# Column tiles of one width in the expert stage, and the groups of experts dealt anew

## The chip, the cores and the metric

One core of one Trainium2 chip runs the whole program. The metric is device time in microseconds, the median of three runs: 1858.34 us (1855.30 to 1859.64) before the change. All times below are us unless marked ns. TensorE (PE) does the matmuls, VectorE (DVE), ScalarE (ACT) and GpSimd (POOL) the rest, and SyncE (SP) issues the transfers from HBM, each engine in the order of its own queue.

## The reference, cut to what matters

The reference is one block of a network on 512 tokens of width 1024: a differential attention and a state-space branch side by side, their merge, and then a mixture of 64 experts. Only the last stage is changed. Every token goes to two experts, and each expert has 6 MB of float32 weights, 402.7 MB in all.

```python
MOE_EXPERTS, MOE_TOP_K, MOE_HIDDEN = 64, 2, 512
g_sel = jnp.argmax(g_logits, axis=-1)                    # one of 8 groups of experts
top_v, top_i = lax.top_k(e_sel_logits, MOE_TOP_K)        # two experts of that group
...
def expert_block(args):
    xblk, e = args
    hid = jax.nn.silu(xblk @ w_gate[e]) * (xblk @ w_up[e])
    return hid @ w_down[e]
...
out = jnp.zeros((n_tok, d), jnp.float32).at[buf_tok].add(yb.astype(jnp.float32) * buf_w[:, None])
return rms_norm(x + out, final_norm_w, NORM_EPS)
```

## The kernel before

The first 850 us are projections, attention and the state-space branch. Then the router runs, and the expert stage follows.

*Slots and groups.* Each expert gets a fixed number of slots, columns of the 128 columns of a tile, for the tokens sent to it. Experts 0 to 2 (`NS = 3`, L1202) keep their place; the other 61 are sorted on the chip by their number of tokens, fullest first, and the sorted order is the table `perm`. Places below `NW = 12` are wide and get 64 slots, the others 32 (`width`, L1214). Experts are dealt into groups that fill 128 slots (L1208 to L1212): the first is `[0, 1]`, two wide ones; then follow 18 groups, of kind T (one wide, two narrow) or F (four narrow) as the string at L1210 says. Tokens beyond an expert's slots would be done in a loop at the end (L1839), which runs as often as the tables of `overflow_tables` (L1646) say.

*One group.* `gather` (L1683) collects the group's tokens with one-hot matmuls, for two groups at a time, after the gate and up projections of every second group. `gate_up` (L1708) runs over eight k (128 rows of the weight each) and two halves (gate, up), and in each such step has one matmul for each expert of the group: the stationary operand is the expert's slots (32 or 64 columns), the moving one 512 columns of its weights. An expert's matmul uses only its own columns of the array. `down` (L1732) does the same over four k and two halves. A float32 matmul stands as two records in the trace. `combine` (L1761) adds the result of the group before into the output rows, and `slots` (L1693) makes the tables that this needs.

*Weights and buffers.* A weight tile is 128 x 2048 float32, 1 MB; an expert has four for gate and up (`gu`) and two for down (`dn`). The list `tiles` (L1223 to L1227) is the order in which they are loaded: by group, and in it all gate and up tiles before the down tiles. `fill` (L1605) issues the next tiles of the list on SP while there is room: 17 buffers of the pool `big`, one `ewx` and one pair of `stg`; from group 1 on two of `big` hold the output rows (`room["big"] -= 2`, L1806). After every second k the group's tiles of these two k are freed, and `fill` runs again. SP issues in that order, and a transfer whose buffer is still in use holds up all behind it.

*The start of the stage.* The weights of experts 0 to 2, 18 tiles, need no routing and are issued while the last projection runs. For all others SP reads the place from `perm` (`source`, L1234), which VectorE writes at the end of the router (L1595). On the way there, `rk` (L1490) builds the first group's one-hot matrix `P0` (L1497), in two rounds of two chunks.

Of the kernel before, what the change touches and what calls it, by code (L numbers as in the profile page):

```python
# [14 lines left out]
OP = mybir.AluOpType  # L15
# [103 lines left out]
def block_kernel(ctx: ExitStack, tc: tile.TileContext, I, out):  # L119
# [1079 lines left out]

    NS, NW = 3, 12  # L1202
    narrow = iter(range(NW, 64))

    def some(n):
        return [next(narrow) for _ in range(n)]

    groups = [[0, 1]]  # L1208
    wide = list(range(2, NW))
    for kind in "TFTFTTFTFTFTTFTFTF":  # L1210
        groups.append([wide.pop(0)] + some(2) if kind == "T" else some(4))
    NG = len(groups)  # L1212

    def width(e):  # L1214
        return 64 if e < NW else 32

    def spans(g_):
        o = 0
# [3 lines left out]

    tiles = []  # L1223
    for g_ in groups:
        first = [e for e in g_ if e < NS]
        for es in (first, g_[len(first):]):
            tiles += [("gu", e, q) for q in range(4) for e in es] + [("dn", e, q) for q in range(2) for e in es]  # L1227
    wt = {}
    nxt = {"i": 0, "end": False}
    LASTN = 4  # L1230
# [212 lines left out]
    def route(cl, prev):  # L1443
        cs = slice(cl[0], cl[-1] + 1)
        n = len(cl)
        g = lambda k: R[k][:, cs]

        def r1():
            gl = lg[:, cs, 0:8]
            first("gm", "og", lambda c: lg[:, c, 0:8], gl)  # L1450

        def r2():
            el = lg[:, cs, 8:72].rearrange("p c (g e) -> p c g e", g=8)
            V.tensor_tensor(R["et"][:, cs], el, og4(cs), op=OP.mult)
            V.tensor_reduce(g("es"), R["et"][:, cs].rearrange("p c g e -> p c e g"), axis=AX.X, op=OP.add)

        def first(m, o, row, rows):
            V.tensor_reduce(g(m), rows, axis=AX.X, op=OP.max)
            for c in cl:
                V.scalar_tensor_tensor(R["d1"][:, c], row(c), R[m][:, c:c + 1], rev8, op0=OP.is_equal, op1=OP.mult)  # L1460
            V.tensor_reduce(g("gx"), g("d1"), axis=AX.X, op=OP.max)
            V.tensor_tensor(g(o), g("d1"), b8(g("gx")), op=OP.is_equal)

        def r3():
            first("m1", "o1", lambda c: R["es"][:, c], g("es"))

        def r4():
            V.scalar_tensor_tensor(g("es"), g("o1"), NEG, g("es"), op0=OP.mult, op1=OP.add)
            first("m2", "o2", lambda c: R["es"][:, c], g("es"))

        def r5():
            V.tensor_tensor(g("d1"), g("o1"), g("o2"), op=OP.add)
            V.tensor_tensor(R["ab"][:, cs], og4(cs), g("d1")[:, :, None, :].to_broadcast([128, n, 8, 8]), op=OP.mult)

        def abf(c):
            return R["ab"][:, c].rearrange("p g e -> p (g e)")

        def rank():
            if cl[0] == 0:
                R["rps"] = side()  # L1480
            rps = R["rps"]
            for c in cl:
                for cc in range(c):
                    T.matmul(rps[:, c * E:c * E + E], lhsT=onesb, rhs=abf(cc), start=(cc == 0), stop=False)
                T.matmul(rps[:, c * E:c * E + E], lhsT=triS, rhs=abf(c), start=(c == 0), stop=True)
            if cl[-1] == NCH - 1:
                for c in range(NCH):
                    T.matmul(rps[:, 256:256 + E], lhsT=onesb, rhs=abf(c), start=(c == 0), stop=(c == NCH - 1))

        def rk():  # L1490
            V.scalar_tensor_tensor(rk1[:, cs].rearrange("p c e -> p (c e)"), R["rps"][:, cl[0] * E:cl[-1] * E + E], 1.0,
                                   R["ab"][:, cs].rearrange("p c g e -> p (c g e)"), op0=OP.add, op1=OP.mult)
            if cl[0] == 0:
                R["P0"] = mt("P", [128, NCH, 256], "P")[:, :, :128]
            for c in cl:
                for e in range(2):
                    V.tensor_scalar(R["P0"][:, c, 64 * e:64 * e + 64], iota1, rk1[:, c, e:e + 1], fst[:, 3, c:c + 1],  # L1497
                                    op0=OP.is_equal, op1=OP.mult)

        def gat(k):  # L1500
            if cl[0] == 0:
                gb[k] = side()
            gather_mm(R["P0"], gb[k][:, :128], k, cl)

        deps = [lgj[c] for c in cl]
        pr = 0.15 if not prev else 0.3
        j = J("V", 1.2, r1, deps + ([rtj] if not prev else []), prio=pr)
        r["gd", cl[0]] = j
        j = J("V", 0.6, r2, [j, r.get("et")], prio=pr)
        r["et"] = j  # L1510
        j = J("V", 1.2, r3, [j], prio=pr)
        j = J("V", 1.4, r4, [j], prio=pr)
        m2j.append(j)
        j = J("V", 0.45, r5, [j], prio=pr)
        kw = None
        if prev:
            kw = J("P", 0.214 * KW, lambda: keep_warm(KW), [lmj[3]], prio=10, acq=["s"], rel=["s"], lag=0.2)
        rj = J("P", 0.1, rank, [j, prev, kw], prio=1, acq=["s"] if not prev else [], lag=0.2)
        if cl[-1] == NCH - 1:
            J("P", 0.9, lambda: keep_warm(4), [rj], prio=1, acq=["s"], rel=["s"])  # L1520
        kj = J("V", 0.2 + 0.35 * n, rk, [rj, r.get("rk")], prio=pr)
        r["rk"] = kj
        last = cl[-1] == NCH - 1
        for k0 in (0, 1):
            j = J("P", 0.22 * n, lambda k0=k0: gat(k0), [kj, lmj[3], r.get(("g", k0))],
                  prio=2 if last else 10, acq=["s"] if not prev else [], lag=0.2)
            r["g", k0] = j
        return rj, kj
# [117 lines left out]
    def overflow_tables():  # L1646

        ex = mt("y", [128, 1024], "ex")
        ext, pe, pf, ef = (ex[:, i * E:i * E + E] for i in range(4))
        io = ex[:, 320:352]  # L1650
        cm = R["cnt"]
        V.tensor_scalar(cm[:, :NW], cm[:, :NW], 64.0, None, op0=OP.subtract)
        V.tensor_scalar(cm[:, NW:], cm[:, NW:], 32.0, None, op0=OP.subtract)
        V.tensor_scalar(ext, cm, 0.0, None, op0=OP.is_gt)
        for m in range(1, 8):
            V.scalar_tensor_tensor(ext, cm, 64.0 * m, ext, op0=OP.is_gt, op1=OP.add)
        a, b = ext, pe
        for sft in (1, 2, 4, 8, 16, 32):
            V.tensor_copy(b[:, :sft], a[:, :sft])
            V.tensor_tensor(b[:, sft:], a[:, sft:], a[:, :E - sft], op=OP.add)  # L1660
            a, b = b, (pf if b is pe else pe)
        V.tensor_scalar(io, iota1[:, :32], -1.0, None, op0=OP.add)
        V.memset(ef, 0.0)
        V.tensor_copy(ef[:, 0:1], a[:, E - 1:E])
        le = mt("y", [128, 16, E], "le")
        bs = R["base"]
        for i in range(2):
            m = slice(16 * i, 16 * i + 16)
            V.tensor_tensor(le, a[:, None, :].to_broadcast([128, 16, E]),
                            io[:, m].unsqueeze(2).to_broadcast([128, 16, E]), op=OP.is_le)  # L1670
            V.tensor_reduce(ef[:, 1 + 16 * i:17 + 16 * i], le, axis=AX.X, op=OP.add)
            V.tensor_tensor(le, le, ext[:, None, :].to_broadcast([128, 16, E]), op=OP.mult)
            V.tensor_reduce(bs[:, m], le, axis=AX.X, op=OP.add)
        em = ef[:, 1:33]
        V.tensor_tensor(bs, io, bs, op=OP.subtract)
        V.tensor_scalar(em, em, float(E - 1), None, op0=OP.min)
        V.tensor_scalar(io, em, NW - 0.5, 32.0, op0=OP.is_lt, op1=OP.mult)
        V.tensor_scalar(io, io, 32.0, None, op0=OP.add)
        V.scalar_tensor_tensor(bs, bs, 64.0, io, op0=OP.mult, op1=OP.add)
        V.tensor_copy(R["ovi"], ef)  # L1680

# [11 lines left out]
    def slots(P, es, wcols):  # L1693
# [11 lines left out]
            V.tensor_scalar(sl[r], ws[r, e:e + 1], 0.5, None, op0=OP.mult)  # L1705
        return pt, sl

    def gate_up(xt, es, gu, done=lambda k: None, pre=lambda k: None):  # L1708
        W = es[-1][1].stop
        pg, pu = gps.tile([128, 512], F32, name="g"), gps.tile([128, 512], F32, name="g")  # L1710
        for k in range(8):
            pre(k)
            for i, o in enumerate((pg, pu)):
                for e, r in es:
                    T.matmul(o[r], lhsT=xt[:, k, r], rhs=gu(e, k)[:, i * 512:i * 512 + 512],  # L1715
                             start=(k == 0), stop=(k == 7), tile_position=(0, r.start))
            done(k)
# [14 lines left out]
    def down(ht, es, dn, done=lambda k: None):  # L1732
        ps = [side(), side()]
        for k in range(4):
            for i in range(2):
                for e, r in es:
                    T.matmul(ps[i][r], lhsT=ht[:, k, r], rhs=dn(e, k)[:, i * 512:i * 512 + 512],  # L1737
                             start=(k == 0), stop=(k == 3), tile_position=(0, r.start))
            done(k)
# [38 lines left out]
    for gi, g_ in enumerate(groups):  # L1778
# [37 lines left out]
        if gi == 3:  # L1816
            overflow_tables()
        pt, sl = ps_
        if gi % 2:
            ps_ = group_slots(P, gi + 1)  # L1820
            if not last and gi + 2 < NG:
                P = onehot(groups[gi + 2:gi + 4])
        elif gi and not last:
            xt = rows(256)
            gather(P, xt)
            ps_ = group_slots(P, gi + 1)
        yps = down(ht, es, wk("dn"), done("dn"))
        if gi == 0:
# [163 lines left out]
```

## Time and profile before

| | |
|---|---|
| median of three runs | 1858.34 us (1855.30 to 1859.64) |
| profiled execution, its own time | 1855.86 us |
| span of that execution | 1854.1 us |
| mean granted clock of TensorE | 0.987 |
| PE busy | 1792.5 us (97%) |
| DVE busy | 794.3 us (43%) |
| ACT busy | 422.2 us (23%) |
| read from HBM | 471.04 MB |

The profile is one execution on the chip. It lists busy times, the span in 40 equal slices of 46.35 us with the busy share in tenths, who waited for whom, and the costliest groups of instructions; the trace behind it gives single instructions and any stretch of time. Matmuls are pipelined, so a busy TensorE is not one at its peak.

### The profile page before, as it was taken

How to read it: one execution, taken by the hardware profiler on the slowest of the kernel's cores; microseconds unless marked ns; L12 is line 12 of the kernel's file. 1: busy time of each engine (PE TensorE's matmuls, PEld its weight loads, DVE VectorE, ACT ScalarE, POOL GpSimd, SP SyncE). 2: the span in 40 equal slices, each digit the busy share in tenths (PEclk: the TensorE clock that was granted, in tenths of full speed). 3: DMA queues.
4: the chain of work that ended last, by engine and by line, in shares of the span. 5: the costliest groups of instructions: out<-in, count | busy, mean ns of one | idle time of the engine just before them, and what ended most of it. 6: DMA issues, size and time to landing. Idle time of an engine off the chain costs nothing. (4 is left out here: it accounts for less than half of the span.)

```text
span 1854.1 us, 23043 instructions
## 1 busy us (share of the span) xinstructions
PE 1792.5 (97%) x8767; PEld 1034.0 (56%) x8767; DVE 794.3 (43%) x1566; ACT 422.2 (23%) x869; POOL 317.6 (17%) x329
## 2 busy tenths in 40 slices
PE   8999999999999999999999999999999999998995
PEld 6877788878787777886424242342424242432432
DVE  7698832587877865324121512121121211212122
ACT  4355530344443432121101010000101010100101
POOL 5244421253635342100000000000000000000001
PEclk8999999999999999999999999999999999999998
DMA  5311122212122123369689999989999999999996
GB/s 158 101 63 52 47 91 91 80 58 91 61 77 74 64 71 100 103 248 367 245 313 421 420 420 420 420 339 421 420 420 420 420 421 415 374 420 420 421 420 255
DMA packets 81472, 474.66 MB, mean 256 GB/s; under 512 B 10192, under 2 KB 10576, under 8 KB 35664
## 3 DMA queue, kind: packets, MB, share of 16 engines
q1 hardware_dynamic: 81360, 473.17, 64.7%
q8 instruction: 70, 1.15, 0.2%
q14 instruction: 42, 0.34, 0.0%
HBM read 471.04 MB, written 2.10 MB: 255 GB/s over the span
## 5 line engine op out<-in xcount | busy, mean ns | idle before, releaser
L1715 PE MATMUL g<-ew,xt 128*32 128x512 f32 (+1 forms) x1904 | 460.3, 603 | 13.4 <-DMA ew<-in_gu_dram 13.3
L243 PE MATMUL g<-hH,w 128*128 128x512 f32 x1024 | 345.7, 401 | 0.0
L1715 PEld LDWEIGHTS g<-ew,xt 128*32 128x32 f32 (+1 forms) x1904 | 91.9, 114 | 348.5 <-issue 319.0
L1737 PE MATMUL s<-ew,hT 128*32 128x512 f32 (+1 forms) x968 | 245.2, 634 | 13.4 <-DMA ew<-in_dn_dram 12.0
L243 PEld LDWEIGHTS g<-hH,w 128*128 128x128 f32 x1024 | 192.4, 188 | 43.7 <-issue 6.0
L243 PE MATMUL g<-hL,w 128*128 128x512 f32 x512 | 199.9, 390 | 0.0
L1720 DVE SCALAR_TENSOR_TENSOR hh<-hh,g 128x512 f32<-128x512 f32 x19 | 13.1, 687 | 407.3 <-ACT hh L1719 407.3
L1894 POOL TENSOR_TENSOR fst<-fst 128x1 f32<-128x1 f32 x4 | 1.2, 302 | 987.8 <-ACT fo L1887 987.6
L203 DVE TENSOR_TENSOR w<-stg,w 128x1024 fp32r<-128x1024 f32 x108 | 141.9, 1322 | 55.4 <-ACT w L200 32.2
L1737 PEld LDWEIGHTS s<-ew,hT 128*32 128x32 f32 (+1 forms) x968 | 49.2, 119 | 193.7 <-issue 150.9
L1436 PE MATMUL s<-P,x 128*128 128x256 f32 (+1 forms) x640 | 136.3, 372 | 0.0
L1436 PEld LDWEIGHTS s<-P,x 128*128 128x128 f32 x640 | 117.3, 192 | 20.8 <-issue 5.7
L1747 DVE SCALAR_TENSOR_TENSOR yl<-s,sl,yh 128x512 fp32r<-128x512 f32 x38 | 28.3, 750 | 201.6 <-ACT yh L1746 201.0
L198 POOL TENSOR_SCALAR w<-stg 128x1024 fp32r<-128x1024 f32 x60 | 70.8, 1180 | 253.9 <-DMA stg<-in_wu_dram 169.8
L1719 ACT ACTIVATE hh<-g 128x512 f32<-128x512 f32 x19 | 11.3, 597 | 425.1 <-PE g L1715 425.1
L243 PEld LDWEIGHTS g<-hL,w 128*128 128x128 f32 x512 | 96.4, 188 | 16.8
L848 DVE SCALAR_TENSOR_TENSOR xb<-u,cw,xb 128x511 f32<-128x511 f32 (+2 forms) x96 | 81.7, 861 | 23.4 <-ACT xb L844 21.7
L1759 DVE TENSOR_TENSOR acc<-acc,s 128x512 f32<-128x512 f32 x144 | 87.6, 679 | 8.1 <-PE s L1754 8.1
L243 PE MATMUL g<-w,hH 128*128 128x512 f32 x256 | 84.5, 411 | 0.0
L1746 ACT ACTIVATE yh<-s,sl 128x512 fp32r<-128x512 f32 x38 | 26.0, 687 | 253.9 <-PE s L1737 253.6
L200 ACT ACTIVATE w<-stg 128x1024 fp32r<-128x1024 f32 x60 | 63.2, 1053 | 75.4 <-DMA stg<-in_wu_dram 52.8
L243 PE MATMUL g<-sH,w 128*128 128x512 f32 x256 | 79.9, 393 | 0.0
(332 smaller groups left out, 2385.6 us busy)
## 6 DMA issues: line engine op xcount, KB each, us to landing
ew<-in_gu_dram SPq DMA_DIRECT2D x238, 1024.0 KB, 17.4
ew<-in_dn_dram SPq DMA_DIRECT2D x117, 1024.0 KB, 17.6
stg<-in_wu_dram SPq DMA_DIRECT2D x120, 512.0 KB, 3.6
stg<-in_gu_dram SPq DMA_DIRECT2D x36, 512.0 KB, 17.3
stg<-in_dn_dram SPq DMA_DIRECT2D x14, 512.0 KB, 17.4
xT<-in_xT_dram SPq DMA_DIRECT2D x4, 512.0 KB, 5.7
x<-in_xn_dram SPq DMA_DIRECT2D x2, 1024.0 KB, 11.2
ew<-in_dn_dram SPq DMA_DIRECT2D x4, 512.0 KB, 13.7
```

Of the source, the lines that this page charges most:

```text
L198: G.tensor_scalar(c["h"], c["st"], 1.0, 0.0, op0=OP.mult, op1=OP.add)
L200: A.activation(c["h"], c["st"], AF.Copy)
L203: (G if i % 10 == 9 else V).tensor_tensor(c["lo"], c["st"], c["h"].bitcast(F32), op=OP.subtract)
L243: T.matmul(cell[b], lhsT=x, rhs=y, start=first and i == 0, stop=last and i == 2)
L848: V.scalar_tensor_tensor(x()[:, 3 - k:], t["u"][:, :n], w[:, k:k + 1], x()[:, 3 - k:], op0=OP.mult, op1=OP.add)
L1436: T.matmul(o, lhsT=x1(c)[:, d], rhs=P[:, c], start=(c == 0), stop=(c == NCH - 1))
L1715: T.matmul(o[r], lhsT=xt[:, k, r], rhs=gu(e, k)[:, i * 512:i * 512 + 512], start=(k == 0), stop=(k == 7), tile_position=(0, r.start))
L1720: V.scalar_tensor_tensor(hh, hh, 1.0, pg[:W], op0=OP.add, op1=OP.mult)
L1737: T.matmul(ps[i][r], lhsT=ht[:, k, r], rhs=dn(e, k)[:, i * 512:i * 512 + 512], start=(k == 0), stop=(k == 3), tile_position=(0, r.start))
L1746: A.activation(yh[:, i], ps[i][:W], AF.Copy, scale=sl[:, :1])
L1747: V.scalar_tensor_tensor(yl[:, i], ps[i][:W], sl[:, :1], yh[:, i].bitcast(F32), op0=OP.mult, op1=OP.subtract)
L1759: V.tensor_tensor(res(c)[:, h], src(c)[:, h], ps, op=OP.add)
```

## The change

Five wide places fewer, and another shape of matmul. `NW` becomes 10, the first group holds experts 0, 1 and 2, of which only expert 0 is wide, and the rest is dealt as seven T and ten F groups, so there are 18 groups instead of 19 and eight wide experts instead of twelve. A new function `parts` cuts every expert's columns into pieces of 32, so a wide expert has two matmuls per step, on the same weights, where it had one; a group always has four matmuls of 32 columns per step. The list of tiles no longer sets the fixed experts apart, the one-hot matrix of the first group is built for three experts, and the overflow tables learn which places are wide. The last group is now one of odd number, so the gather ahead of it is for one group alone.

```diff
-    NS, NW = 3, 12
+    NS, NW = 3, 10
...
-    groups = [[0, 1]]
-    wide = list(range(2, NW))
-    for kind in "TFTFTTFTFTFTTFTFTF":
+    groups = [[0, 1, 2]]
+    wide = list(range(NS, NW))
+    for kind in "FTFTFFTFTFFTFTFTF":
         groups.append([wide.pop(0)] + some(2) if kind == "T" else some(4))
...
     def width(e):
-        return 64 if e < NW else 32
+        return 64 if e == 0 or NS <= e < NW else 32
...
     for g_ in groups:
-        first = [e for e in g_ if e < NS]
-        for es in (first, g_[len(first):]):
-            tiles += [("gu", e, q) for q in range(4) for e in es] + [("dn", e, q) for q in range(2) for e in es]
+        tiles += [("gu", e, q) for q in range(4) for e in g_] + [("dn", e, q) for q in range(2) for e in g_]
...
             for c in cl:
-                for e in range(2):
-                    V.tensor_scalar(R["P0"][:, c, 64 * e:64 * e + 64], iota1, rk1[:, c, e:e + 1], fst[:, 3, c:c + 1],
+                for e, r_ in spans(groups[0]):
+                    V.tensor_scalar(R["P0"][:, c, r_], iota1[:, :width(e)], rk1[:, c, e:e + 1], fst[:, 3, c:c + 1],
                                     op0=OP.is_equal, op1=OP.mult)
...
-        V.tensor_scalar(cm[:, :NW], cm[:, :NW], 64.0, None, op0=OP.subtract)
-        V.tensor_scalar(cm[:, NW:], cm[:, NW:], 32.0, None, op0=OP.subtract)
+        V.tensor_scalar(cm, cm, 32.0, None, op0=OP.subtract)
+        for a_, b_ in ((0, 1), (NS, NW)):
+            V.tensor_scalar(cm[:, a_:b_], cm[:, a_:b_], 32.0, None, op0=OP.subtract)
...
+    def parts(es):
+
+        return [(e, slice(o, o + 32)) for e, r in es for o in range(r.start, r.stop, 32)]
+
     def gate_up(xt, es, gu, done=lambda k: None, pre=lambda k: None):
...
-                for e, r in es:
+                for e, r in parts(es):
                     T.matmul(o[r], lhsT=xt[:, k, r], rhs=gu(e, k)[:, i * 512:i * 512 + 512],
                              start=(k == 0), stop=(k == 7), tile_position=(0, r.start))
...
-                for e, r in es:
+                for e, r in parts(es):
                     T.matmul(ps[i][r], lhsT=ht[:, k, r], rhs=dn(e, k)[:, i * 512:i * 512 + 512],
                              start=(k == 0), stop=(k == 3), tile_position=(0, r.start))
...
-        if gi % 2:
+        if gi % 2 and not last:
             ps_ = group_slots(P, gi + 1)
-            if not last and gi + 2 < NG:
+            if gi + 2 < NG:
                 P = onehot(groups[gi + 2:gi + 4])
         elif gi and not last:
             xt = rows(256)
-            gather(P, xt)
+            gather(P, xt[:, :, :P.shape[2]])
             ps_ = group_slots(P, gi + 1)
```

Where instructions stand, at three places. On SP, the loads around the first read of `perm` (`TENSOR_LOAD`); `ISA` sets an address, `ew` and `stg` are weight tiles. Before:

```order
L192 DMA stg<-in_wu_dram 128x1024 x3
L1270 DMA ew<-in_gu_dram 128x2048 x5
L1268 DMA stg<-in_gu_dram 128x1024 x2
L1270 DMA ew<-in_gu_dram 128x2048
L1270 DMA ew<-in_dn_dram 128x2048 x4
L1270 DMA ew<-in_gu_dram 128x2048 x4
L1270 DMA ew<-in_dn_dram 128x2048 x2
L1238 TENSOR_LOAD perm
```

After, at the same place:

```order
L192 DMA stg<-in_wu_dram 128x1024 x3
L1268 DMA ew<-in_gu_dram 128x2048 x5
L1266 DMA stg<-in_gu_dram 128x1024 x2
L1268 DMA ew<-in_gu_dram 128x2048 x5
L1268 DMA ew<-in_dn_dram 128x2048 x6
L1236 TENSOR_LOAD perm
```

With the one tile issued earlier both have 18 tiles ahead of the first read of `perm`; expert 2's gate and up tiles have moved ahead of the down tiles of experts 0 and 1.

On TensorE, the end of the gate and up projections of group 1 and the start of the combine. Before, a T group:

```order
L1715 MATMUL g<-ew,xt 64x512
L1715 MATMUL g<-ew,xt 32x512
L1715 MATMUL g<-stg,xt 32x512
L1753 MATMUL s<-yh,pt 128x512
L1754 MATMUL s<-yl,pt 128x512
```

After, an F group:

```order
L1721 MATMUL g<-ew,xt 32x512 x3
L1721 MATMUL g<-stg,xt 32x512
L1721 MATMUL g<-ew,xt 32x512 x32
L1759 MATMUL s<-yh,pt 128x512
L1760 MATMUL s<-yl,pt 128x512
```

Three matmuls a step, one of them 64 columns wide, have become four of 32.

On VectorE, the last round of `rk` and the count that starts the sorting. Before:

```order
L1589 TENSOR_TENSOR gd<-lg,gm 128x32
L1491 SCALAR_TENSOR_TENSOR ptab<-s,ab 128x128
L1497 TENSOR_SCALAR P<-iota_93,ptab,fst 128x64 x4
L1557 COPY cnt<-s 128x64
L1558 SCALAR_TENSOR_TENSOR ox<-cnt,ox 128x64
```

After:

```order
L1489 SCALAR_TENSOR_TENSOR ptab<-s,ab 128x128
L1495 TENSOR_SCALAR P<-iota_93,ptab,fst 128x64
L1495 TENSOR_SCALAR P<-iota_93,ptab,fst 128x32 x2
L1495 TENSOR_SCALAR P<-iota_93,ptab,fst 128x64
L1495 TENSOR_SCALAR P<-iota_93,ptab,fst 128x32 x2
L1555 COPY cnt<-s 128x64
```

Four pieces ahead of the count have become six.

## Rows read from the trace of the kernel before

**Rows 1.** The page, part 2: the span in 40 slices of 46.35 us.

```profile
PE   8999999999999999999999999999999999998995
DMA  5311122212122123369689999989999999999996
GB/s 158 101 63 52 47 91 91 80 58 91 61 77 74 64 71 100 103 248 367 245 313 421 420 420 420 420 339 421 420 420 420 420 421 415 374 420 420 421 420 255
```

**Rows 2.** Windows: length, busy us per engine (records), granted clock, DMA share, GB/s.

```profile
862.00:869.00 7.00, 6.65 (x38) 3.15 (x39) 3.29 (x19) 0.94 (x3) 0.00 (x0) 0.92 0.58 204
869.00:905.00 36.00, 35.31 (x185) 20.42 (x185) 5.62 (x19) 6.31 (x14) 0.00 (x0) 1.00 0.90 349
905.00:920.00 15.00, 15.00 (x61) 6.98 (x60) 2.57 (x6) 2.87 (x6) 0.00 (x0) 1.00 0.00 1
920.00:936.00 16.00, 16.00 (x51) 2.70 (x50) 0.00 (x0) 0.00 (x0) 0.00 (x0) 1.00 1.00 394
936.00:964.00 28.00, 28.00 (x107) 8.75 (x110) 11.23 (x29) 1.88 (x3) 0.00 (x0) 1.00 0.67 256
964.00:1206.00 242.00, 236.92 (x1091) 88.77 (x1080) 63.34 (x146) 22.09 (x40) 0.00 (x0) 1.00 1.01 419
1206.00:1226.00 20.00, 20.00 (x77) 7.78 (x76) 1.31 (x5) 1.45 (x4) 0.00 (x0) 1.00 0.59 233
1226.00:1576.00 350.00, 340.16 (x1514) 120.26 (x1513) 68.58 (x147) 28.76 (x51) 0.00 (x0) 0.98 1.01 419
1576.00:1596.00 20.00, 19.75 (x90) 4.96 (x92) 7.34 (x23) 1.97 (x3) 0.00 (x0) 1.00 0.83 314
1596.00:1828.00 232.00, 219.95 (x1110) 82.27 (x1098) 44.81 (x89) 19.06 (x34) 0.00 (x0) 0.99 1.02 419
1828.00:1834.00 6.00, 5.17 (x24) 1.32 (x24) 0.60 (x1) 0.69 (x1) 0.00 (x0) 1.00 0.62 227
```

**Rows 3.** The page, part 6: gate and up tiles, KB each, us to landing.

```profile
ew<-in_gu_dram SPq DMA_DIRECT2D x238, 1024.0 KB, 17.4
```

**Rows 4.** Timeline of TensorE: start, us, operation, tiles, shape, records; three groups.

```profile
862.99 1.98 PE L1715 MATMUL g<-ew,xt 128*64 128x512 f32 x8
...
865.98 1.94 PE L1715 MATMUL g<-ew,xt 128*64 128x512 f32 x8
...
888.86 7.09 PE L1737 MATMUL s<-ew,hT 128*64 128x512 f32 x32 [0.69 <-ACT hT L1729]
...
978.12 0.50 PE L1753 MATMUL s<-yh,pt 128*128 128x512 f32 x1
...
982.59 14.08 PE L1436 MATMUL s<-P,x 128*128 128x256 f32 x64
...
997.88 7.07 PE L1737 MATMUL s<-ew,hT 128*32 128x512 f32 x64
...
1540.07 31.83 PE L1715 MATMUL g<-ew,xt 128*64 128x512 f32 x96
```

**Rows 5.** Windows of 2 us around the first gap of the stream.

```profile
918.00:920.00 2.00, 2.00 (x7) 0.34 (x6) 0.00 (x0) 0.00 (x0) 0.00 (x0) 1.00 0.00 0
920.00:922.00 2.00, 2.00 (x7) 0.34 (x6) 0.00 (x0) 0.00 (x0) 0.00 (x0) 1.00 0.90 274
```

**Rows 6.** Timeline of VectorE on the way to the expert order.

```profile
859.62 0.98 DVE L1497 TENSOR_SCALAR P<-iota,ptab,fst 128x64 f32<-128x64 f32 x4
...
861.03 0.17 DVE L1559 TENSOR_SCALAR ox<-ox 128x3 f32<-128x3 f32 x1
...
863.42 0.20 DVE L1595 CAST perm<-s 1x64 int32<-1x64 f32 x1
```

**Rows 7.** Waits of the SP queue, 855 to 870: us in total, times, longest.

```profile
SPq L1238 <- DVE perm L1595: 13.3, 1, 13.3
```

**Rows 8.** Windows of 2 us where TensorE waits for weights and works again.

```profile
1464.00:1466.00 2.00, 1.40 (x2) 0.00 (x0) 0.00 (x0) 0.00 (x0) 0.00 (x0) 0.50 1.00 416
...
1472.00:1474.00 2.00, 1.97 (x4) 0.25 (x4) 1.45 (x2) 0.69 (x1) 0.00 (x0) 1.00 1.03 430
```

More of the change, by code (lines that the diff above doesn't have):

```diff
@@ L1676, in overflow_tables @@
         V.tensor_scalar(em, em, float(E - 1), None, op0=OP.min)
-        V.tensor_scalar(io, em, NW - 0.5, 32.0, op0=OP.is_lt, op1=OP.mult)
-        V.tensor_scalar(io, io, 32.0, None, op0=OP.add)
+        nb = ex[:, 352:384]
+        V.tensor_scalar(nb, em, NS - 0.5, None, op0=OP.is_lt)
+        V.scalar_tensor_tensor(nb, em, 0.5, nb, op0=OP.is_gt, op1=OP.mult)
+        V.scalar_tensor_tensor(io, em, NW - 0.5, nb, op0=OP.is_lt, op1=OP.subtract)
+        V.tensor_scalar(io, io, 32.0, 32.0, op0=OP.mult, op1=OP.add)
         V.scalar_tensor_tensor(bs, bs, 64.0, io, op0=OP.mult, op1=OP.add)
```

## The prediction

> **What bounds the kernel now.** Start with the slices. From slice 18 on the DMA row stands at 9 in almost every slice and the GB/s row at 420, and that stretch is the expert stage, 1 ms long [rows 1]. In the same slices TensorE reads 9 too, so the page alone does not say which of the two is the bound. The windows say it [rows 2]. In three long stretches (964 to 1206, 1226 to 1576, 1596 to 1828 us) the DMA engines move 419 GB/s, share 1.01 to 1.02, however much TensorE does beside it. I take 419 GB/s as the rate of a full stream. A weight tile is 1024 KB [rows 3], 1.0486 MB, so one tile takes 1.0486/0.419 = **2.50 us**.
>
> Between those stretches the stream is short of work. The stream time lost in a stretch is its length x (1 - rate/419). From the rows in order [rows 2]: 862 to 869: 3.6 us; 869 to 905: 6.0; 905 to 920: 15.0; 920 to 936: 1.0; 936 to 964: 10.9; 1206 to 1226: 8.9; 1576 to 1596: 5.0; 1828 to 1834 (the small last pieces): 2.7. That is 53.1 us, and it closes: 862 to 1834 is 972 us, less 53.1 is 919, and by the names of the tiles the 366 still to come at 862, with the half-tile of `finw`, need 366.5 x 2.50 = 916. So the end of this kernel is "stream start + 916 us + lost stream time + the 20 us after the last weight". The first 3.6 us (the stream has nothing to load until the expert order is known) and the last 2.7 stay. **46.8 us** lie in the middle, and are what a change can win.
>
> Why they are lost: the stream stops when every buffer holds a tile that TensorE has not used. There are 19 places (17 of `big`, one `ewx`, one pair of `stg`), 17 from group 1 on, when `acc` takes two. Two kinds of work fill the gap between one release and the next. A group of four 32-column experts takes 7.07 us for the 64 records of a down projection, twice that for gate and up, about 21.2 us in all [rows 4]. A group with one 64-column and two 32-column experts takes 31.83 us for 96 records of gate and up [rows 4], so about 47.7 in all, although it uses a quarter fewer tiles: per step of k and output half 1.99 us against 0.88. Two 64-column tiles alone are no slower than four of 32: 7.09 us for the first group's down projection [rows 4]. It is the mixture that costs.
>
> **The change, part by part.**
>
> *The order of the first loads.* Eighteen tiles are asked for before the expert order is known, before and after, and a nineteenth once it is. What changes is who frees them. Group 0 steps through two k in 865.98 - 862.99 = 2.99 us each, 6.0 us for a pair [rows 4]. Before, a pair frees two tiles, 5.0 us of stream; 5.0/6.0 is 0.83, and the row says 349/419 = 0.83 [rows 2]. After, group 0 has three experts and a pair frees three tiles, 7.5 us of stream for 6.0 us of time. The stream no longer starves there: the 6.0 us come back. TensorE's own time in group 0 I leave as it is: 64+32+32 columns as four tiles should take what two tiles of 64 took, since four 32s take 7.07 and two 64s 7.09 [rows 4].
>
> *The gap at 905 to 920.* By the end of group 0, 18 places are free rather than 12. From 869 the stream has 18 tiles, 45 us, to 914. The next release: gate and up of group 1 start where they start now, about 911 (the gather in between, some 14 us, is the same [rows 4]), and two steps of k of a four-expert group take 4 x 0.88 = 3.5 us instead of 7.9, so about 915. Today the stream restarts 1.6 us after its release (911.2 + 7.9 = 919.1; the window 920 to 922 moves 274/419 of 2 us, so data from 920.7) [rows 5]. So 914 to 917 stays idle, about **2.7 us of loss** where 16.0 were (905 to 936).
>
> *936 to 964, 1206, 1576.* The first is group 1, today a mixed group that releases three tiles in 7.9 us; it becomes four tiles in 3.5 us. The other two are the places where two mixed groups stand behind each other. After, every group is four tiles wide and takes 21.2 us of matmuls, and the longest stretch without a release is combine, gather, slots and half a down projection: 997.88 - 978.12 + 3.5 = 23.3 us [rows 4]. The 17 places hold 17 x 2.50 = 42.5 us of stream. TensorE's whole need is 18 x (21.2 + 3.9 combine + 2.0 transposes and slots) + 8 x 14.1 + 7 for gathers = 608 us against 916 of stream. So from 917 the stream should never stop: 24.8 us come back.
>
> *Added.* VectorE builds the first one-hot matrix in 12 pieces instead of 8; the last two chunks lie on the way to the expert order, which SP waits for [rows 6, 7]. Four 64-column pieces take 0.98 us [rows 6]; two of 64 and four of 32 take at least 2 x 0.245 + 4 x 0.17 (if 32 columns cost what the shortest neighbours do) and at most 6 x 0.245, so +0.2 to +0.5; I take **+0.4**, nearer the upper end, since a piece of three columns still takes 0.17. The load of the expert order on SP, the first ordered tile and all behind it move by that. The extra VectorE lines in the overflow tables lie in group 3, beside gathers, and nobody waits for them. The removed nineteenth group takes one combine and half a gather off TensorE, which has slack. In the mixed groups TensorE gets 128 matmul records for 96.
>
> *Capacity.* Experts 1 and 2 now hold 32 tokens, and seven sorted experts hold 64. Routing the reference's own input by hand gives 35, 20 and 9 tokens to the fixed three and 39, 37, 33, 28 to the fullest others, so no token overflows before or after, and the loop at the end runs zero times.
>
> *Sum.* 46.8 - 2.7 - 0.4 = **43.7 us** off. The profiled execution took 1855.86 us (span 1854.1), so 1812.2; it is 2.5 below the median of 1858.34, which gives **1814** for a median.
>
> All of this hangs on the rate of the full stream, which is 419 GB/s for 350 us at a stretch [rows 2]. The Trainium skill, "DMA: Bandwidth & Descriptors", section Specifications, gives about 358 GB/s as what HBM can give one core; by it the 384.3 MB would need 1073 us, 157 more than here, and the time would be near 1970. The trace does not agree, the kernel before could not have ended at 1854 by it, so the measured rate stands.
>
> **The rivals.**
>
> *The clock falls while TensorE waits.* When the stream rules, TensorE gets one matmul per landing tile and then waits. The rows show what that does: with two records in 2 us the granted clock goes to 0.50 (1464 to 1466, the 1.2 GHz level), and once work is dense it is back at 1.00 by 1472 [rows 8]. The Trainium skill, "TensorE: Matmul & The Clock Gate", section on HAM oscillation, says that a kernel whose matmul bursts are shorter than its DMA waits runs its bursts at the low clock each time; by that rule, the trace agrees for the waits, and shows the return during dense work. Mild form: gathers and combines also run at half speed, the stretch without releases is 46.6 us instead of 23.3, 4 us beyond the buffers, in each of 8 even groups: 33 us lost, **1847**. Full form, the one that ends slower than before: the clock stays at 0.50 for the whole stage, TensorE needs 1216 us, and the end is 300 us later than forecast, near **2110**. It decides from the point where 608/clock exceeds 963 us, the stream's 916 plus today's 46.8, a mean clock below 0.63. Against it: when TensorE becomes the bound it has dense work, and the rows show the clock back at 1.00 soon after work is dense [rows 8].
>
> *The two half tiles do not run side by side.* They read the same weight tile as moving operand; no row shows two column tiles doing that. If the pair costs what a 64-column tile costs today, a mixed group stays at 47.7 us. TensorE then needs 608 + 7 x 26.5 = 794 us, still below 916, and a mixed group with its follower takes about 95 us against 105 of stream, so the middle would be fine. Only the start would show it, since group 0 is mixed itself: its k pairs take 10 us for 7.5 of stream. The first release comes 4 us later, 2.6 us of stream are empty behind each of three pairs, 4 before the first release of the down projection, and group 1 begins 25 us later, with 11 us of empty stream before its first release. That is 27 us of loss for 2.7: **1838**. For it: nothing but that it is unseen. Against: four tiles with four moving operands share the array at 0.44 us a set.
>
> **How the numbers follow.** Forecast 0.80; half tiles not side by side 0.08; low clock, mild 0.06; low clock, full 0.06 (a third of it near break-even). The range: the floor is all 46.8 and half of the 3.6 us won, and three runs that fall as far below 1858 as the lowest of before did (3 us), 1806; the ceiling is the forecast plus an early gap as large as today's 936 to 964 (11 us) plus up to 4 us if the last projection and combine run at 0.50: 1829. It leaves out the 0.20 of the rivals. A measurement here tells about 0.2% from no change: faster 0.94, within it 0.02, slower 0.04.
>
> **What would show it.** Right: GB/s near 420 from about 917 to the end with no dip; mixed groups with 0.44 us a set of four; TensorE waiting for ew tiles in every group; the last weight landing near 1790; a granted clock well below today's 0.987, with gathers at 1.00. Wrong: a dip of several us in the gathers of even groups (low clock), or mixed groups still at 1.98 us a step (half tiles in turn).

## The result and the profile after

The changed kernel takes **1815.27 us** (median; 1812.63 to 1816.23). The kernel before, run beside it, took 1858.24 (1855.3 to 1859.64). The ratio is 0.9769, with a 95% interval of 0.9752 to 0.9785. That is 43.0 us less, for a forecast of 1814 and a term of 43.7. The same kernel taken twice more, each time beside the kernel before, gave 1812.93 (after_again, ratio 0.9745) and 1815.35 (after_third, 0.976). Of wide places it has eight for twelve, so four fewer, not five.

The profiled execution of after took 1816.23 us, with a span of 1814.4. First its page: TensorE, its granted clock (PEclk, in tenths), the DMA engines and GB/s in 40 slices of 45.4 us, and the row of the gate and up matmuls (busy us, mean ns of one, idle us ahead of them and what ended it).

```profile
PE   8999999999999999999999778797887879788786
PEclk8999999999999999999999999899998999899998
DMA  5311122222221213349899999999999999999995
GB/s 162 103 59 43 63 82 85 90 70 70 70 82 48 92 47 107 103 147 397 358 396 420 419 421 420 421 420 420 421 419 421 420 420 421 419 420 420 421 420 228
...
L1721 PE MATMUL g<-ew,xt 128*32 128x512 f32 x2152 | 387.7, 678 | 138.8 <-DMA ew<-in_gu_dram 138.1
```

The dips to 339, 374 and 313 GB/s of [rows 1] are gone: from slice 21 (counted from 0) to the last but one the stream holds 419 to 421. TensorE, which stood at 9 there, now mostly reads 7 and 8, and waits 138.1 us for gate and up tiles. In these slices the bound is now the stream alone, and it is a stream without holes.

Next, the stretches of [rows 2] for after (length, busy us per engine with records, granted clock, DMA share, GB/s):

```profile
862.00:869.00 7.00, 6.63 (x35) 2.84 (x38) 3.94 (x21) 1.20 (x4) 0.00 (x0) 0.58 0.51 187
869.00:905.00 36.00, 35.31 (x276) 18.83 (x269) 5.79 (x20) 5.76 (x13) 0.00 (x0) 1.00 0.94 386
905.00:920.00 15.00, 15.00 (x107) 9.71 (x110) 2.72 (x7) 3.53 (x7) 0.00 (x0) 1.00 0.93 367
920.00:936.00 16.00, 16.00 (x128) 7.47 (x124) 8.27 (x21) 1.19 (x2) 0.00 (x0) 1.00 1.00 400
936.00:964.00 28.00, 21.02 (x150) 5.59 (x142) 3.58 (x10) 1.38 (x2) 0.00 (x0) 0.94 1.02 422
964.00:1206.00 242.00, 199.10 (x1123) 88.36 (x1124) 62.71 (x141) 21.80 (x40) 0.00 (x0) 0.93 1.01 420
1206.00:1226.00 20.00, 19.75 (x159) 7.92 (x157) 2.66 (x6) 2.32 (x4) 0.00 (x0) 1.00 1.02 421
1226.00:1576.00 350.00, 281.55 (x1659) 117.23 (x1660) 72.25 (x166) 27.98 (x50) 0.00 (x0) 0.94 1.02 420
1576.00:1596.00 20.00, 14.14 (x82) 2.92 (x81) 2.17 (x3) 1.38 (x2) 0.00 (x0) 0.91 1.02 419
1596.00:1780.00 184.00, 151.80 (x926) 64.36 (x918) 34.41 (x65) 15.05 (x29) 0.00 (x0) 0.93 1.01 420
1780.00:1790.00 10.00, 7.57 (x52) 2.07 (x52) 0.00 (x0) 0.60 (x1) 0.00 (x0) 1.00 0.87 322
```

By length x (1 - rate/420) the losses are 3.9 (862 to 869), 2.9 (to 905), 1.9 and 0.8 (to 936), then almost nothing until 1780, and 2.3 in the ten us ahead of 1790. The three stretches 936 to 964, 1206 to 1226 and 1576 to 1596, which lost 10.9, 8.9 and 5.0 before, lose nothing.

Last, TensorE's timeline in groups 0 to 3 (start, us, operation, tiles, shape, records, idle before and what ended it):

```profile
863.70 3.64 PE L1721 MATMUL g<-ew,xt 128*32 128x512 f32 x16
...
868.64 1.92 PE L1721 MATMUL g<-ew,xt 128*32 128x512 f32 x16
...
891.46 7.07 PE L1743 MATMUL s<-ew,hT 128*32 128x512 f32 x64 [0.69 <-ACT hT L1735]
...
913.75 4.06 PE L1721 MATMUL g<-ew,xt 128*32 128x512 f32 x35
...
1018.92 6.57 PE L1721 MATMUL g<-ew,xt 128*32 128x512 f32 x26 [1.44 <-DMA ew<-in_gu_dram]
```

The first two rows and the third are group 0, which holds the split 64-column expert: 64 records of down take 7.07 us, exactly what four 32-column experts take in [rows 4], and a step of gate and up takes 1.92 us, except the first one. The last row is a step of group 3 behind waits for weights.

### The profile page after: what moved, and what is told of

Read it like the earlier page. It is cut to its first block, busy times and chain, and to the rows that moved or that the text cites. A ratio compares the mean times of both kernels' runs of the same rounds, so it can differ in the third digit from the quotient of the medians.

```text
span 1814.4 us, 23712 instructions
## 1 busy us (share of the span) xinstructions
PE 1621.2 (89%) x9119; PEld 1012.8 (56%) x9119; DVE 782.7 (43%) x1544; ACT 418.6 (23%) x865; POOL 316.3 (17%) x329
## 5 line engine op out<-in xcount | busy, mean ns | idle before, releaser
L1721 PE MATMUL g<-ew,xt 128*32 128x512 f32 x2152 | 387.7, 678 | 138.8 <-DMA ew<-in_gu_dram 138.1
L1721 PEld LDWEIGHTS g<-ew,xt 128*32 128x32 f32 x2152 | 90.6, 121 | 410.9 <-DMA ew<-in_gu_dram 250.4
L1743 PE MATMUL s<-ew,hT 128*32 128x512 f32 x1096 | 153.9, 620 | 19.1 <-DMA ew<-in_dn_dram 17.6
L1434 PE MATMUL s<-P,x 128*128 128x256 f32 (+1 forms) x640 | 130.6, 363 | 0.3 <-DVE P L1495 0.2
L1434 PEld LDWEIGHTS s<-P,x 128*128 128x128 f32 x640 | 112.6, 192 | 21.6 <-issue 6.7
L1743 PEld LDWEIGHTS s<-ew,hT 128*32 128x32 f32 x1096 | 40.7, 113 | 116.1 <-issue 73.2
L848 DVE SCALAR_TENSOR_TENSOR xb<-u,cw,xb 128x511 f32<-128x511 f32 (+2 forms) x96 | 81.7, 861 | 23.4 <-ACT xb L844 21.7
L1765 DVE TENSOR_TENSOR acc<-acc,s 128x512 f32<-128x512 f32 x136 | 82.7, 678 | 15.7 <-PE s L1760 15.7
L1721 PE MATMUL g<-stg,xt 128*32 128x512 f32 x152 | 73.9, 685 | 1.5 <-DMA stg<-in_gu_dram 1.3
## 6 DMA issues: line engine op xcount, KB each, us to landing
ew<-in_dn_dram SPq DMA_DIRECT2D x117, 1024.0 KB, 19.1
```

The costliest lines, as they stand in the source:

```text
L848: V.scalar_tensor_tensor(x()[:, 3 - k:], t["u"][:, :n], w[:, k:k + 1], x()[:, 3 - k:], op0=OP.mult, op1=OP.add)
L1434: T.matmul(o, lhsT=x1(c)[:, d], rhs=P[:, c], start=(c == 0), stop=(c == NCH - 1))
L1765: V.tensor_tensor(res(c)[:, h], src(c)[:, h], ps, op=OP.add)
```

## The experiments

Where only the time counts, a run is compared with the kernel before of its own job. For the steps inside, this table takes two points of each profiled execution: the VectorE copy of the expert order (`perm`), from which the ordered tiles can be asked for, and the first of the eight small matmuls (line 303) that follow the last weight. The time between them is the stream with all its losses. The last column is TensorE's idle time ahead of the final combine.

```
run               order ready   weights used   between   idle ahead of last combine
before               863.42        1835.03      971.6      1.75
after                864.14        1795.48      931.3      1.75
after_again          864.49        1793.48      929.0      1.82
after_third          861.73        1791.07      929.3      1.82
e1_whole             866.22        1821.29      955.1      1.76
e2_split_only        862.19        1805.36      943.2      4.90
e3_mixed_first       863.33        1791.51      928.2      1.81
e4_gather_twice      864.52        1806.28      941.8      1.80
e5_gather_thrice     864.76        1901.75     1037.0      1.75
e6_fourth_fixed      861.63        1790.25      928.6      1.81
e7_early_group1      864.54        1790.67      926.1      5.27
e8_early_only        864.93        1791.81      926.9      5.32
e9_shifted_code      864.25        1790.34      926.1      2.25
```

The expert order is ready up to 3 us earlier or later from one execution to the next, also of one kernel (861.73 to 864.49 for after). That is 2.8 of the 4.2 us between the three profiled executions of after. In e6, e7 and e9 the first tile behind the 18 does not wait for that order, so their "between" is to be compared with care.

**One part alone: the new groups with whole 64-column tiles (e1_whole).**

```diff
-        return [(e, slice(o, o + 32)) for e, r in es for o in range(r.start, r.stop, 32)]
+        return es
```

> The changed grouping, but a 64-column expert runs as one tile of 64 columns again. Theory (release of buffers at the start of the stage, stream full later): a mixed step of k and half is back at 1.99 us, TensorE needs about 794 us against 916 of stream, and since no two mixed groups stand behind each other the stream stays full at 420 GB/s from about 942 on; only the start loses, some 27 us between 862 and 942. 1838 us (1830 to 1846). Rival (mixed groups bind the stage wherever they stand): dips of 5 to 10 us at most of the seven mixed groups, 1850 or more, near the kernel before.

Measured: 1842.24 us (1837.0 to 1844.46), ratio 0.9905 (0.9881 to 0.9929), 27.0 above after. The windows of its start, and from TensorE's timeline the first step of group 0 and a later one piece by piece:

```profile
862.00:869.00 7.00, 5.59 (x26) 2.28 (x27) 5.89 (x31) 0.94 (x3) 0.00 (x0) 1.00 0.52 187
869.00:905.00 36.00, 36.00 (x148) 12.07 (x146) 0.73 (x2) 4.00 (x9) 0.00 (x0) 1.00 0.74 288
905.00:920.00 15.00, 14.31 (x56) 3.71 (x52) 5.14 (x19) 0.60 (x1) 0.00 (x0) 1.00 0.79 299
920.00:936.00 16.00, 16.00 (x69) 11.10 (x68) 0.00 (x0) 2.84 (x6) 0.00 (x0) 1.00 0.80 312
936.00:964.00 28.00, 28.00 (x227) 13.25 (x229) 13.06 (x34) 3.30 (x6) 0.00 (x0) 1.00 0.71 276
964.00:1206.00 242.00, 222.92 (x1052) 79.30 (x1044) 58.13 (x133) 19.13 (x34) 0.00 (x0) 0.98 1.02 420
```

```profile
865.69 4.04 PE L1721 MATMUL g<-ew,xt 128*64 128x512 f32 x12
...
886.36 1.07 PE L1721 MATMUL g<-stg,xt 128*64 128x512 f32 x2
887.36 1.05 PE L1721 MATMUL g<-ew,xt 128*32 128x512 f32 x4
888.34 1.07 PE L1721 MATMUL g<-stg,xt 128*64 128x512 f32 x2
```

Twelve records in 4.04 us where after needs 1.92 for sixteen: the mixture of tile widths costs its 2 us per step and output half here too. The later step shows how: the 64-column tile runs for 1.00 us, and only then the two 32-column tiles, for 0.98. Tiles of two widths stand one behind the other, where four of one width run side by side. The losses up to 964 are 3.9 + 11.3 + 4.3 + 4.1 + 9.6 = 33.2 us, against 9.5 in after: 23.7 of the 27. From 964 on there is no dip (418 to 420 GB/s in every window from there to 1780), although all seven other mixed groups come there, the first from 966.46. With whole tiles the mixture hurts only where group 0 has to feed the stream; later, with TensorE's surplus, the places cover it. A mixture that was dear in the kernel before is nearly free in another grouping.

**The other part alone: the old groups with split tiles (e2_split_only).** The lines of before, and in `gate_up` and `down`:

```diff
-                for e, r in es:
+                for e, r in parts(es):
```

> The old grouping (first group of two wide experts, 18 more, ten of them mixed), with every wide expert split into two tiles of 32 columns. Theory: the dips at 936 to 964, 1206 and 1576 go (24.8 us), the starving in group 0 stays (two tiles freed per 6.0 us, 6.0 us lost), and the gap before group 1's first release shrinks from 16 to about 11.5 us, because a pair of k there takes 3.5 us instead of 7.9. 28 us off, 1830 us (1824 to 1838). Rival (the regrouping carries the gain, the split little): 1845 or more, with the dips still there.

Measured: 1833.65 us (1830.79 to 1833.89), ratio 0.9864 (0.9848 to 0.9881), 18.4 above after. Its windows:

```profile
869.00:905.00 36.00, 35.30 (x263) 20.65 (x256) 5.63 (x19) 6.22 (x13) 0.00 (x0) 1.00 0.88 341
905.00:920.00 15.00, 15.00 (x125) 7.45 (x127) 2.57 (x6) 2.58 (x5) 0.00 (x0) 1.00 0.37 141
920.00:936.00 16.00, 16.00 (x128) 7.53 (x124) 10.48 (x28) 1.19 (x2) 0.00 (x0) 1.00 1.02 422
...
964.00:1206.00 242.00, 207.31 (x1265) 91.20 (x1264) 60.82 (x144) 23.50 (x43) 0.00 (x0) 0.94 1.02 420
```

The losses at 869 to 920 stay, 6.8 + 10.0 us: with two experts in group 0, a pair of k frees two tiles and 12 places are full too early. Behind 920 nothing is lost any more (419 to 422 GB/s in every window to 1780). The table gives 12 us over after for the stream (14 over its two repeats), and 3 more us in its last column; experiment e8 shows what those are.

The table's gains of the two parts, 16.5 us (e1) and 28.4 (e2), nearly sum to the 40.3 to 42.6 of the whole, but by chance, for the parts are not separate. The dips at 1206 and 1576, 13.9 us, go in e1 and go in e2 too: split tiles remove them, and so does a grouping in which no two mixed groups stand behind each other. They are counted twice. At the start it is the other way round: up to 964 the kernel before loses 36.5 us, e1 33.2, e2 20.3 and after 9.5. The third expert in group 0 gains little as long as its group runs unsplit, and both parts together win more there than the two alone.

**The order of the groups (e3_mixed_first).**

```diff
-    for kind in "FTFTFFTFTFFTFTFTF":
+    for kind in "TFFTFFTFTFFTFTFTF":
```

> The changed kernel with the first two groups after group 0 exchanged: a mixed group stands first. Theory (with four tiles of 32 columns both kinds cost TensorE the same): group 1's first release gives one tile to the stream instead of two, later ones three per 3.5 us, still more than the 2.5 us a tile that the stream takes; 1 to 3 us more than the changed kernel, 1816 to 1818. Rival (a mixed group first is what made the early losses): 10 us or more lost between 905 and 964, 1825 or above.

Measured: 1814.44 us (1812.41 to 1817.15), ratio 0.9765 (0.9748 to 0.9783), the same as after, and not the 1 to 3 us more that I expected. With split tiles a mixed group behind group 0 costs nothing that these runs can tell.

**How much slack the stream's cover has (e5_gather_thrice, e4_gather_twice).** The gather in even groups from 2 on lies in the longest stretch in which TensorE frees no place. It is done three times, then twice, with the same result.

```diff
             gather(P, xt[:, :, :P.shape[2]])
+            gather(P, xt[:, :, :P.shape[2]])
+            gather(P, xt[:, :, :P.shape[2]])
```

> The changed kernel with every gather of an even group from group 2 on done three times (same result, 28 us more of TensorE each). Theory (the stream stops when the stretch without a release outlasts the buffers): 23.3 + 28.2 = 51.5 us against 17 x 2.50 = 42.5, about 9 us and a restart of 1.6 lost in each of seven groups, 1875 to 1892, with gaps of about 10 us in GB/s behind each gather. Rival (only TensorE's total counts: 608 + 7 x 28.2 + 14 = 819 us, still under 916): 1815, no gaps.

Measured: 1924.28 us (1922.49 to 1925.76), ratio 1.0354 (1.0336 to 1.0372), 109 above after. TensorE's timeline of e5 in group 2, then windows around it:

```profile
962.85 3.62 PE L1721 MATMUL g<-ew,xt 128*32 128x512 f32 x26 [1.44 <-DMA ew<-in_gu_dram]
...
970.86 41.71 PE L1434 MATMUL s<-P,x 128*128 128x256 f32 x192
```

```profile
1000.00:1004.00 4.00, 4.00 (x21) 3.51 (x20) 0.00 (x0) 0.95 (x2) 0.00 (x0) 1.00 0.84 350
1004.00:1008.00 4.00, 4.00 (x20) 3.54 (x19) 0.00 (x0) 1.42 (x3) 0.00 (x0) 1.00 0.02 8
...
1012.00:1016.00 4.00, 4.00 (x39) 2.34 (x41) 1.31 (x5) 0.47 (x1) 0.00 (x0) 1.00 0.02 4
1016.00:1020.00 4.00, 4.00 (x44) 1.25 (x40) 0.00 (x0) 0.00 (x0) 0.00 (x0) 1.00 0.66 173
```

The stream stops at about 1003.3 (350/420 of the first window) and comes back at about 1018.4 (173/420 of the last): 15.1 us. The trace has seven such stops, one for each gather of two groups; the eighth gather, ahead of the last group, is for one group alone, and there is none. 109/7 is 15.6 each. The rival, that only TensorE's total counts, falls: it had no gaps and 1815. But the price is far above my figure of about 10.6 us a group, and the rows say why. TensorE begins on the last gate and up tile at 962.85. By the stop at 1003.3 less 17 x 2.50 us, its data had landed at 960.8, some 2 us earlier, and from there on the stream lives on its 17 places, not from the end of the matmuls. The same working gives 1.8 to 2.3 us at six of the seven stops; the landing of a single tile is not shown by itself.

> The changed kernel with every gather of an even group from group 2 on done twice (same result, 14.1 us more of TensorE each, 106 us in all). Theory (release window): 23.3 + 14.1 = 37.4 us, still inside the 42.5 us that the buffers hold, so the added 106 us of TensorE cost 0 to 3 us: 1815 to 1818. Rival (TensorE is still half the bound): 10 us or more slower than the changed kernel.

Measured: 1828.80 us (1826.21 to 1829.76), ratio 0.983 (0.9816 to 0.9843), 15.9 above after_again, which ran beside it and took 1812.93 us (1811.07 to 1815.26), ratio 0.9745 (0.9731 to 0.9758). I expected at most 3 us, so this expectation failed, and the size is the rival's. Its reason is not: most of the loss stands as gaps in the stream near the gathers. The windows of the same group:

```profile
1004.00:1008.00 4.00, 4.00 (x44) 1.29 (x40) 0.04 (x1) 0.69 (x1) 0.00 (x0) 1.00 0.95 339
1008.00:1012.00 4.00, 4.00 (x44) 1.18 (x36) 1.46 (x2) 0.69 (x1) 0.00 (x0) 1.00 1.00 392
```

One us is lost here; by the table it is 12.8 in all over after_again, 1.8 for each of seven gathers. So one gather more (14.1 us) just passes the edge, and the slack of after is about 12 us, not the 19 of the prediction.

**The remaining hole at 914 (e6_fourth_fixed, e7_early_group1).** In e6 group 1 begins with a fourth expert that needs no expert order, so that one more tile is known early; e7 is e6 with a gather of 128 columns ahead of group 1 and the other 128 behind its gate and up projection.

```diff
-    NS, NW = 3, 10
+    NS, NW = 4, 11
...
+    groups.append([3] + some(3))
...
+            if gi == 1:
+                gather(P[:, :, 128:], xt[:, :, 128:])
...
-            gather(P, xt)
+            gather(P[:, :, :128], xt[:, :, :128])
```

> The changed kernel with a fourth expert that keeps its place (32 slots, in group 1), so that the nineteenth tile is known before the expert order is and loads ahead of it. Theory (stream time lost between 862 and 870 counts in full): one tile, 2.5 us less, about 0.14%: 1811.5 to 1813. Rival (the start is hidden behind the first release anyway): same as the changed kernel.

Measured: 1813.26 us (1811.09 to 1815.1), ratio 0.975 (0.9736 to 0.9763); after_again, beside it, 1812.93. No gain, where I expected 2.5 us. The tile loads early, but the stream then stands still until the first release (0 GB/s from 864 to 866): all 19 places are full either way. What limits the start is places, not knowledge of the next expert.

> As the one before, and the gather ahead of group 1 collects group 1's 128 columns alone (9.3 us for 14.1), group 2's follow after group 1's gate and up. Theory: group 1's first release comes 4.8 us earlier, which closes the rest of the gap at 914 to 917 (1.9 to 2.7 us): 4 to 5 us less than the changed kernel, 1809 to 1811. Rival: nothing beyond the one before.

Measured: 1815.92 us (1813.44 to 1820.46), ratio 0.9765 (0.9751 to 0.978). No gain either, where I expected 4 to 5 us, and yet the hole is closed, as e7's windows show:

```profile
905.00:920.00 15.00, 15.00 (x136) 5.04 (x135) 3.06 (x8) 1.34 (x3) 0.00 (x0) 1.00 1.01 418
920.00:936.00 16.00, 16.00 (x130) 12.35 (x133) 9.61 (x26) 3.53 (x9) 0.00 (x0) 1.00 1.02 420
```

The table has the stream 2.5 us shorter than in e6 (926.1 for 928.6), and the last column has 3.5 us more.

**Where the gain of e7 went (e8_early_only, e9_shifted_code, after_third).** e8 is after with the early gather alone. e9 is e7 with 24 small matmuls that nobody reads, in group 10, where TensorE waits for weights anyway; they move all its later code.

```diff
+        if gi == 10:
+            keep_warm(24)
```

> The changed kernel, with only group 1's 128 columns gathered ahead of group 1 and the other 128 after its gate and up projection; no fourth fixed expert. Theory (the time is stream start + stream need + lost stream + tail): the gate and up projection of group 1 starts about 7 us earlier, before the places are full, so the 2.7 us lost between 905 and 936 come back: 420 GB/s from 905 on, and a time 2 to 3 us under the changed kernel of the same job, ratio near 0.973 to before. Rival (the end is set by something behind the stream): the stream closes its gap and the time stays within 1 us of the changed kernel, as the run with the fourth fixed expert did; then the chain of waits shows TensorE standing about 4.4 us without a releaser ahead of the last combine, as there.

> The kernel with the fourth fixed expert and the early gather of group 1, and 24 small matmuls without a reader put into group 10, where TensorE waits for weights; they move the code of TensorE behind them. Theory (the 4.37 us without a releaser ahead of the last combine hang on where the code behind the empty loop lies): the stand falls back to about 0.9 us, the time 3 to 4 us under the run without the shift, near 1812. Rival (it hangs on what the kernel does there, not on where its code lies): the stand stays at 4.4 us and the time at 1815 to 1816.

> The changed kernel again, as the measure for the two beside it: 1811 to 1817, and about 0.9 us without a releaser ahead of the last combine.

Measured: e8 1817.01 us (1816.51 to 1817.58), ratio 0.9766 (0.9753 to 0.978); e9 1812.90 (1808.59 to 1813.96), 0.9742 (0.9726 to 0.9758); after_third 1815.35 (1811.99 to 1817.29), 0.976 (0.9747 to 0.9774). For each, the piece of the chain that ended last just ahead of the final combine (start, us, what), in the order e8, e9, after_third:

```profile
1793.86 4.43 issue
```

```profile
1792.39 1.36 issue
```

```profile
1793.12 0.94 issue
```

The rival of e8 holds: the hole is closed, as e8's window shows, and the time isn't better, with a stand of 4.43 us in which TensorE waits for nothing that semaphores show.

```profile
905.00:920.00 15.00, 15.00 (x139) 5.08 (x138) 3.09 (x8) 1.74 (x3) 0.00 (x0) 1.00 1.01 418
```

The theory of e9 holds as far as one kernel can show it: code moved by 24 matmuls, and the stand is down to 1.36. The traffic of the DMA queue of kind "instruction" fits. In e8 between 1792 and 1798, then in after_third between 1790 and 1794 (packets, MB, share):

```profile
q8 instruction: 2, 0.03, 2.1%
```

```profile
q8 instruction: 1, 0.02, 1.9%
```

Between the last weight and the final combine lies the loop for overflowing tokens, which runs zero times, so by the program TensorE jumps over it. In after_third one packet lands in that time, and the combine starts 0.4 us later. In e8 two packets land, 3 us apart, and the combine starts 0.4 us behind the second. e7 and e2 show two as well, with stands of 4.37 and 4.01 us; each of the other kernels shows one, with 0.86 to 1.36. So the 4 us are read as code that has to be loaded in two steps when the jump's target lies badly. That reading is argued: which engine's code a packet holds is not in the view, and the place of the code was moved only once. After such a stand the combine's first matmuls take 0.63 us instead of 0.39, with the granted clock at 0.50 in e8. They do so in after_again and e4 too, behind a stand of 0.9, so the stand alone does not decide it. From "weights used" to the end of the span it is 19.0 us in after_third, 20.0 in after_again and 23.4 to 24.0 in e2, e7 and e8: about 1 us for the slow clock alone, 4.4 to 5.0 with the long stand.

No version clearly beats after. e9 has, with e7, the shortest stream, and it has the lowest ratio, but its interval overlaps that of after_third.

## Why the prediction was right

**The law held.** "Stream start + 916 us + lost stream + tail" accounts for every run above, with one term that I had taken as fixed: counted from "weights used", the tail is 19 to 20 us in most kernels and 23 to 24 in e2, e7 and e8. The full stream ran at 419 to 422 GB/s wherever TensorE left it places, in all kernels, so the measured rate stood. The figure of the Trainium skill, "DMA: Bandwidth & Descriptors", section Specifications, about 358 GB/s for one core (there a stack's 716 GB/s shared between two), is not borne out by any run here, where one core runs alone.

**Group 0.** I gave back all 6.0 us of 869 to 905. In the profiled execution 2.9 of them stayed: its first step took 3.64 us instead of 1.92 (rows above), with the granted clock at 0.58 in 862 to 869, so the first release came 1.7 us late. The two repeats show 412 and 421 GB/s in this stretch at a granted clock of 1.00, so there the term is right. Why the clock fell in one execution and not in the others, the traces don't show. By the table, the profiled execution's stream is 2.0 to 2.3 us longer than that of the repeats.

**The gap at 905 to 936.** Predicted 2.7, measured 1.9 + 0.8 = 2.7, and 2.6 in both repeats. Gate and up of group 1 start at 913.75, where I had said about 911; in this execution the stream ran late as well, so the gap came out the same. e7 and e8, which start them earlier, close it.

**936 on.** Predicted 24.8 us back; all of it came. The 10.9 us at 936 to 964 come back with the split alone (e2), not with the regrouping alone (e1 loses 9.6 there); for the 13.9 at 1206 and 1576 either part is enough.

**The 0.4 us on VectorE.** The six pieces now take 1.37 us:

```profile
859.96 1.37 DVE L1495 TENSOR_SCALAR P<-iota,ptab,fst 128x64 f32<-128x64 f32 x6
```

Against 0.98 us for four in [rows 6], that is +0.39. In the time it can't be seen: the expert order moves by 3 us from one execution to the next.

**The mis-sized step.** The longest stretch without a release, 23.3 us against 42.5 us of places, measured badly. The stretch must be counted for the stream, not for TensorE: from the landing of the last gate and up tile, some 2 us before TensorE begins on it (worked out above), over its last step (3.62 us), to the first new data after the release (1.6 us later). 23.3 + 2.0 + 3.6 + 1.6 is about 30 us, which leaves 12 and not 19. It changed nothing in after, since both are above zero, but I priced e4 and e5 by it: 0 to 3 us for the 15.9 of e4, and about 10.6 a gap for the 15.1 of e5.

**The end.** I kept 2.7 us for the small last pieces, as before. That was too little: summed the same way over the last 24 us up to "weights used", the stream loses 4.2 us in the kernel before and 6.6 to 6.8 in after and its repeats. So the end costs some 2.5 us more than before, which the prediction had put at nothing; why the stream runs at some 300 GB/s there was not tried. By the table the stream gained 40.3 us, and 42.3 and 42.6 in the repeats, for the 44.1 forecast (43.7 and the 0.4): the end accounts for the repeats, and the slow first step of group 0 for the rest. The tail behind it stayed (19.1 us before, 18.9 after).

**The rivals.** *Half tiles in turn:* refuted by 1.92 us for the 16 records of a step and 7.07 for 64; two column tiles do share the array with the same weights as moving operand. The rival's price was near: e1, where they are not split, took 1842 for the 1838 that I gave. *Low clock:* it does fall, as forecast, and it costs the stream nothing. The windows of after behind the wait at 1018.92, whose step is in the timeline above:

```profile
1019.00:1022.00 3.00, 3.00 (x16) 0.71 (x20) 0.00 (x0) 0.00 (x0) 0.00 (x0) 0.50 1.00 415
1022.00:1025.00 3.00, 3.00 (x14) 0.55 (x6) 0.03 (x1) 0.60 (x1) 0.00 (x0) 0.52 1.04 431
1025.00:1029.00 4.00, 4.00 (x18) 2.96 (x17) 3.90 (x7) 0.00 (x0) 0.00 (x0) 1.00 1.01 420
```

The granted clock is 0.50 (1.2 GHz) in the step behind the waits, which then takes 6.57 us for 26 records where another such step takes 3.62, and it is back at 1.00 for the combine. Of the 427 windows of 2 us from 926 to 1780, 50 have a clock below 0.7, and in none of the 427 does the stream move less than 397 GB/s. Where the low clock meets the final combine, no stream hides it: there it cost 1 us (after_again). The Trainium skill, "TensorE: Matmul & The Clock Gate", section on HAM oscillation, describes this for bursts between DMA waits, and the trace agrees; but the DMA row stays at 415 to 431 GB/s, because the places cover the 3 us. The mean granted clock is 0.96 for 0.987 before.

## What to carry to other kernels

Where a profile shows TensorE and the stream both near full, divide the span into stretches and give each its stream loss; the sum says what a change can win. Take the parts of a change one by one as well, but don't add them up blindly: here two parts removed the same dips, and the start needed both. Count a buffer's cover from the landing of its last tile to the first new data after the release, not from the consumer's first to last instruction. When a hole is closed and the time doesn't move, look at the chain of waits behind the stream before giving up the hole: here a stand of TensorE behind a jump, most likely the loading of code, took back what the stream had gained.

## What the runs showed of the hardware

- A group of four column tiles costs 0.44 us a set whether they read four weight tiles or three; 64 and 32 columns in one group cost 4.04 us for 12 records against 1.92 for 16 (e1, after). The Trainium skill, "TensorEngine Tiling (Array Packing)", section Key Properties, says that a change of tiling mode drains TensorE. The rows of e1 agree with that, since the 32-column tiles begin only when the 64-column one is done; how much of the 2 us is the drain itself they don't separate.
- The places of the stream hide TensorE's low clock: steps at 0.50 behind waits for weights (6.57 us for 3.62), and 415 to 431 GB/s beside that step.
- Where TensorE passes an empty loop it stood for 0.86 to 1.36 us in the kernels in which one packet on the instruction queue landed meanwhile, and for 4.01 to 4.43 where two did, 3 us apart.
